# The first stages of an encoder layer: a buffer claimed at once, sums copied ahead of squares, first half blocks interleaved, late transposes on another engine

## The chip, the cores and the metric

The kernel runs on one core of one Trainium2 chip. The metric is device time in microseconds (us) of one execution. The core has TensorE (PE in the profile; its weight loads are PEld), VectorE (DVE), ScalarE (ACT), GpSimd (POOL) and SyncE (SP), each with its own instruction stream, and 16 DMA engines. SP's stream issues nearly all the loads and many stores; POOL's stream issues other stores and small memsets.

## The reference

One encoder layer over 1024 positions of width 2048, in float32, batch 1:

```python
mod = silu(c) @ w_ada + b_ada
shift, scale, gate = split(mod, 3)
h = rmsnorm(x, pre_g) * (1.0 + scale) + shift
q, k, v, gate_a, u, gate_p = split(h @ w_in)
y_a = windowed_gqa(q, k, v, rel_table, sink) * silu(gate_a)
y_p = multiscale_pool(u, w_pool_grp, pool_scale) * silu(gate_p)
g_a, g_p = split(sigmoid(h @ w_merge + b_merge), 2)
o = (g_a * (y_a @ w_br_attn) + g_p * (y_p @ w_br_pool)) @ w_out
return x + gate * rmsnorm(o, post_g)
```

Only the path to the first columns of `h @ w_in` matters here: the factors of rmsnorm (one per row of x), the scale and the shift (one per column of x), and the first block products.

## The kernel before

**Products.** A float32 operand is split in a high and a low part (`whi`, `wlo`; B11h, B11l and so on), and a product is hi by hi, lo by hi and hi by lo, three matmuls of 128x128 by 128x512. Most of the kernel computes blocks of 256 columns with seven products instead of eight (`strassen`, L212; its matmuls are at L237): the products X, V, Z and others are read from PSUM (the accumulators' memory) by ACT or DVE into sums of the same names.

**The ramp.** The first eight blocks of columns of `w_in` are computed from the first half of x's columns (k-tiles 0 to 3, two pairs j = 0 and 1) before the rest is ready. Blocks 0 to 3 are plain: each has four quarters "11", "21", "12" and "22" (first digit: half of the block's columns; second: half of the rows of x), and each quarter six matmuls per j (`plain_block`, L805, matmuls PB at L814). Their results are copied to `held` tiles (`hold`) or to `c` tiles (`put_by`, L825) and stored to `ramp_d` in DRAM, `held` by SP (`store_held`, L823), `c` by POOL. Blocks 4 to 7 go through `strassen` (`ramp_gen`).

**What comes ahead of the products.** x arrives as `xt` tiles by rows and is transposed on PE (`turn_part`, XT at L486); the transposes are taken from PSUM by `take_turned` (ACT at L494, or DVE). `raw_operands` makes the operands B11h and so on of transposed x with the column factors, in which the row factors and the shift are still missing. The column factors come from sums over `w_ada` on PE (`row_sums`, GEMV at L523; the loads `ada` at L546), whose result ACT copies to `acc` (L527); PE transposes `acc` (PM at L507), and DVE makes `modc`. `modulation` (GEMV at L583) does the same for later columns.

**Row factors.** `square_of` squares a part of x's rows and sums it into `ssq_x`, on ACT (L446) or DVE. `factors` makes `rstd` from the sums, DVE makes eight diagonal pieces `diag` of it, PE spreads them over partitions (RB at L474), and ACT copies the result to `rb` (L475). With `rb` DVE makes the shift-free sums (`sums_unshifted`, L688; `sums_over`), and `put_shifted` adds the shift: from there on the operands are those of h.

**What sets the order.** Instructions that pass through `keep` stand on their engine in the order of the program; a scheduler places the others between them. Tiles of a pool share buffers: the pool `xa` has five buffers of one tag, for which `rb`, four `held` tiles and later `ada` tiles ask. A buffer goes to a tile at its first writing in the scheduled order, not where the tile is named; a tile that gets a used buffer waits until the last use of the old tile is over. A memset of one element by POOL is the kernel's way of claiming a buffer early. In `run`, the steps of the list `at` are called at the given product of a strassen block; `side` steps (here `late_sums`) after products by their count.

The steps around `rb` in the main program, in their order: `factors()`, `put_by(2, "11")`, `low = [wide_weights(3, j) ...]`, `whole_block(2, "21")`, `put_by(2, "21")`, `whole_block(2, "12")`, `spread_factors(low)`, `put_by(2, "12")`, `scale_row` of 0 to 3, block 3 "11", `sums_unshifted()`, block 3 "21", the row sums of the shifts, `sums_over()`, block 2 "22", and then the column step `g[4]()` of the shifts with PM.

Of the kernel before, what the change touches and what calls it, by code (L numbers as in the profile page):

```python
# [15 lines left out]
AF = mybir.ActivationFunctionType  # L16
# [27 lines left out]
def encoder_layer(ctx: ExitStack, tc: tile.TileContext, x, c, table, w_ada, b_ada, pre_g,  # L44
# [409 lines left out]
    rb = xa.tile([P, 2, 512], F32, tag="xa", name="rb")  # L454
    held = {(i, nt): xa.tile([P, 2, 512], F32, tag="xa", name=uid("held")) for i in range(2) for nt in "12"}
# [7 lines left out]
    def spread_factors(then):  # L463
        diags = []
        for s in range(2):
            diags.append(ev.tile([P, 512], F32, tag="ev", name=uid("diag")))
            for m in range(4):
                keep(nc.vector.tensor_scalar(diags[s][:, m * P:(m + 1) * P], ident, rstd[:, 4 * s + m:4 * s + m + 1],
                                             None, op0=ALU.mult))
        for step in then:  # L470
            step()
# [321 lines left out]
    def wide_weights(i, j):  # L793
# [3 lines left out]
        keep(nc.scalar.activation(hi, src, AF.Copy))  # L797
# [7 lines left out]
    def plain_block(i, blk, j, tag=None):  # L805
# [4 lines left out]
        if j == 0:  # L810
            opened[i, blk] = bank(tag, "PB")
        for n in range(6):
            kh, w, m = ((0, whi, 0), (0, wlo, 0), (1, whi, 0), (1, wlo, 0), (0, whi, 1), (1, whi, 1))[n]
# [41 lines left out]
    def turn_next(tags):  # L855
        s, ks = rounds.popleft()
        turn_part(s, ks, tags)
        return [partial(take_turned, s, k, False) for k in ks]
# [11 lines left out]
    low00 = wide_weights(0, 0)  # L870
    g[4]()
    low00()
# [4 lines left out]
    plain_block(0, "11", 0, "sc")  # L877
    plain_block(0, "21", 0, "sc")
    turn_part(1, (0, 1), ("at", "at"))
    raw_operands(0, 1, True)  # L880
    for k in range(2):
        take_turned(1, k, k == 1)
    plain_block(0, "12", 0, "mm")
    plain_block(0, "22", 0, "mm")
# [6 lines left out]
    for si in range(8):  # L891
        square_of(si, 0, si % 2 == 1)
# [6 lines left out]
    raw_operands(1, 1)  # L899
    keep(nc.scalar.activation(ep.tile([P, 1], F32, name="root"), eps_t, AF.Sqrt))  # L900
# [37 lines left out]
    factors()  # L938
    put_by(2, "11")
# [4 lines left out]
    spread_factors(low)  # L944
# [37 lines left out]
    late_takes = [turn_next(("sc", "sc")), turn_next(("at", "at"))]  # L982
# [41 lines left out]
    for n, i in enumerate(range(AHEAD_PAIRS, RAMP)):  # L1024
        at = [(1, partial(second_raws, n - 2))] if n > 1 else []
        if n == 0:
            at.extend(((1, lambda: ramp_raws(7, (0, 1))), (2, partial(take_late, 0)), (3, fill_last),
                       (4, partial(take_late, 1))))
# [930 lines left out]
```

## Time and profile before

| what | value |
|---|---|
| median of 3 runs | 2104.43 us (2101.16 to 2106.51) |
| profiled execution | 2103.02 us, its span 2101.2 us |
| mean clock granted to TensorE | 0.997 |
| PE busy | 2074.6 us, 99% |
| DVE busy | 1557.0 us, 74% |
| ACT busy | 1112.0 us, 53% |
| POOL busy | 42.7 us, 2% |
| DMA | 227 GB/s mean over the span |

The span runs from the first to the last instruction that the profile shows. A row of an engine gives its start, its length, line, operation, output and inputs, their shape, and how often it stands in a row; the bracket at its end is the idle time ahead of it and what ended that. In the chain of waits each step is followed back to what released it. The clock is given as a share of full speed.

### The profile page before, as it was taken

The page shows a single profiled execution, that of the slowest core. Times are in us where ns is not written, and L with a number is a line of the kernel's source. Part 1 is how long each engine was busy: PE and PEld are TensorE (multiplying, and loading weights), DVE is VectorE, ACT ScalarE, POOL GpSimd, SP SyncE. Part 2 cuts the span into 40 slices and gives each one's busy share as a digit, 9 for nine tenths or more (in the row PEclk, how much of TensorE's full clock was granted, in tenths as well). Part 3 has the DMA queues.
Part 4 walks back from the last instruction along what each step waited for, and adds up shares of the span by engine and source line. Part 5 has one row for each costly group of instructions (what it writes and reads, how often), then busy time and mean ns, then how long its engine had stood idle before and what let it go on. Part 6 is the DMA issues. An engine that isn't in the chain of part 4 may idle for free.

```text
span 2101.2 us, 29057 instructions
## 1 busy us (share of the span) xinstructions
PE 2074.6 (99%) x9524; PEld 1704.4 (81%) x9524; DVE 1557.0 (74%) x2804; ACT 1112.0 (53%) x2122; POOL 42.7 (2%) x142
## 2 busy tenths in 40 slices
PE   8899999999999999999999999999999999999998
PEld 5578888788888888888888888888888888888886
DVE  5589777777456776777777678857857977889667
ACT  5574444444574634666665444333645645768654
POOL 1100000000000000000000000010000000000000
PEclk9999999999999999999999999999999999999999
DMA  9868787897575467654544577675755566786896
GB/s 350 308 220 291 261 256 227 282 297 252 170 249 187 151 226 265 223 173 157 187 165 154 165 232 233 213 241 173 251 159 172 171 199 200 231 302 206 295 337 244
DMA packets 303393, 476.62 MB, mean 227 GB/s; under 512 B 24322, under 2 KB 140650, under 8 KB 303240
## 3 DMA queue, kind: packets, MB, share of 16 engines
q1 hardware_dynamic: 297616, 459.89, 66.6%
q0 software_dynamic: 4560, 12.75, 1.6%
q10 hardware_dynamic: 1064, 2.11, 0.3%
q8 instruction: 75, 1.23, 0.3%
q14 instruction: 78, 0.64, 0.1%
HBM read 346.70 MB, written 130.05 MB: 227 GB/s over the span
## 4 chain that ended last, share of the span: by engine, by line
PE 93%; DMA 3%; DVE 2%; ACT 1%; issue 0%; POOL 0%; DVEq 0%; ACTq 0%; SPq 0%; POOLq 0%
PE Z L237 31%; PE X L237 20%; PE V L237 20%; PE Z L1666 2%; PE Z L1668 2%; PE Z L1667 2%; PE X L1666 1%; PE V L1666 1%; PE V L1668 1%; PE X L1668 1%; PE X L1667 1%; PE V L1667 1%; PE PT L1376 1%; PE PB L814 1%; PE PV L1387 0%; DMA xt<-in_x_dram 0%
## 5 line engine op out<-in xcount | busy, mean ns | idle before, releaser
L96 ACT ACTIVATE whi<-raw 128x512 fp32r<-128x512 f32 (+1 forms) x528 | 314.9, 601 | 490.7 <-PE Z L237 249.8
L97 DVE TENSOR_TENSOR wlo<-raw,whi 128x512 fp32r<-128x512 f32 (+1 forms) x528 | 340.2, 650 | 150.3 <-PE Z L237 109.6
L97 DVE TENSOR_TENSOR wlo<-wr,whi 128x512 fp32r<-128x512 f32 x224 | 150.9, 689 | 52.4 <-ACT whi L96 49.4
L96 ACT ACTIVATE whi<-wr 128x512 fp32r<-128x512 f32 x224 | 138.6, 629 | 86.4 <-DVE wlo L97 30.8
L103 DVE TENSOR_TENSOR raw<-raw,raw 128x512 f32<-128x512 f32 x76 | 52.5, 691 | 91.9 <-DMA raw<-in_w_merge_dram 60.2
L96 ACT ACTIVATE whi<-ws 128x512 fp32r<-128x512 f32 (+1 forms) x88 | 53.0, 603 | 74.0 <-PE X L237 60.0
L237 PE MATMUL V<-T4h,whi 128*128 128x512 f32 x328 | 89.4, 391 | 2.0 <-ACT whi L96 2.0
L237 PE MATMUL Z<-T1h,whi 128*128 128x512 f32 x328 | 90.3, 392 | 0.8 <-ACT u L251 0.8
L237 PE MATMUL Z<-B22h,whi 128*128 128x512 f32 x328 | 89.9, 392 | 0.0
L237 PE MATMUL X<-B21h,whi 128*128 128x512 f32 x328 | 89.6, 391 | 0.1
L237 PE MATMUL V<-T3h,whi 128*128 128x512 f32 x328 | 89.5, 391 | 0.2 <-ACT c L828 0.2
L237 PE MATMUL X<-B11h,whi 128*128 128x512 f32 x328 | 89.6, 391 | 0.0
L237 PE MATMUL Z<-T2h,whi 128*128 128x512 f32 x328 | 89.0, 390 | 0.4 <-ACT Z L293 0.3
L237 PE MATMUL X<-B11l,whi 128*128 128x512 f32 x328 | 89.1, 390 | 0.0
L237 PE MATMUL Z<-T2h,wlo 128*128 128x512 f32 x328 | 88.9, 390 | 0.2 <-DVE wlo L97 0.2
L237 PE MATMUL V<-T4h,wlo 128*128 128x512 f32 x328 | 89.0, 390 | 0.0
L237 PE MATMUL Z<-T1l,whi 128*128 128x512 f32 x328 | 89.0, 390 | 0.0
L237 PE MATMUL Z<-B22l,whi 128*128 128x512 f32 x328 | 88.9, 390 | 0.0
L237 PE MATMUL X<-B21l,whi 128*128 128x512 f32 x328 | 88.9, 390 | 0.0
L237 PE MATMUL V<-T3l,whi 128*128 128x512 f32 x328 | 88.9, 390 | 0.0
L237 PE MATMUL X<-B11h,wlo 128*128 128x512 f32 x328 | 88.8, 390 | 0.0
L237 PE MATMUL V<-T4l,whi 128*128 128x512 f32 x328 | 88.8, 390 | 0.0
(418 smaller groups left out, 4913.4 us busy)
## 6 DMA issues: line engine op xcount, KB each, us to landing
part<-part_d SPq DMA_DIRECT2D x136, 256.0 KB, 4.8
ada<-in_w_ada_dram SPq DMA_DIRECT2D x128, 256.0 KB, 5.1
raw<-in_w_merge_dram SPq DMA_DIRECT2D x64, 512.0 KB, 5.4
wr<-ws_dS SPq DMA_DIRECT2D x60, 512.0 KB, 5.2
raw<-in_w_in_dram SPq DMA_DIRECT2D x56, 512.0 KB, 4.3
wr<-in_w_out_dram SPq DMA_DIRECT2D x48, 512.0 KB, 5.1
proj_d<-part SPq DMA_DIRECT2D x68, 256.0 KB, 2.4
sw<-in_w_out_dram SPq DMA_DIRECT2D x64, 256.0 KB, 4.9
```

Source lines behind the costliest of these rows:

```text
L96: ins = (nc.scalar.activation(hi, src, AF.Copy), nc.vector.tensor_tensor(lo, src, f32(hi), ALU.subtract))
L97: nc.vector.tensor_tensor(lo, src, f32(hi), ALU.subtract))
L103: return (eng or nc.vector).tensor_tensor(o, a, b, ALU.add)
L237: nc.tensor.matmul(ps, w_[:, i], op[mov][j][m_], start=fresh and i == 0 and n == 0, stop=i == nj - 1 and n == 2, skip_group_check=True)
L814: keep(nc.tensor.matmul(opened[i, blk], w[:, kh, nt * P:(nt + 1) * P], mov[kh][m], start=j == n == 0, stop=j == 1 and n == 5, skip_group_c ...
L1376: nc.tensor.transpose(pt[:, i * P:(i + 1) * P], p[:, i * P:(i + 1) * P], ident)
L1666: nc.tensor.matmul(pb, hi, w[0], start=first, stop=False, skip_group_check=True)
L1667: nc.tensor.matmul(pb, lo, w[0], start=False, stop=False, skip_group_check=True)
L1668: nc.tensor.matmul(pb, hi, w[1], start=False, stop=last, skip_group_check=True)
```

## The change

A memset of one element by POOL claims `rb`'s buffer ahead of the four `held` tiles. The diagonals are made right behind `factors()`, half of them by ACT. The first `whi` is made by DVE. `plain_block` takes a list of its matmuls (`part`) and has another order of them; the first two pairs of quarters of block 0 are interleaved, with the third part of the first pair behind the transposes of the second half of the rows. Of the squares ahead of the second scale's sums, those of row tiles 2 to 7 move behind `raw_operands(1, ...)`. The late transposes are taken by DVE, and the steps `take_late` and `fill_last` of the ramp's first strassen block move from the products 2, 4 and 3 to 4, 5 and 6.

```diff
@@ -452,6 +452,7 @@
         square_of(si, 1, by_vector, xts[si, 2 + by_vector])
 
     rb = xa.tile([P, 2, 512], F32, tag="xa", name="rb")
+    nc.gpsimd.memset(rb[:, 0, 0:1], 0.0)
     held = {(i, nt): xa.tile([P, 2, 512], F32, tag="xa", name=uid("held")) for i in range(2) for nt in "12"}
 
     def factors():
@@ -460,15 +461,19 @@
         keep(nc.scalar.activation(t[:, 1], t[:, 0], AF.Sqrt, bias=eps_t, scale=1.0 / D))
         keep(nc.vector.reciprocal(rstd, t[:, 1]))
 
-    def spread_factors(then):
-        diags = []
+    diags = []
+
+    def factor_diagonals():
         for s in range(2):
             diags.append(ev.tile([P, 512], F32, tag="ev", name=uid("diag")))
             for m in range(4):
-                keep(nc.vector.tensor_scalar(diags[s][:, m * P:(m + 1) * P], ident, rstd[:, 4 * s + m:4 * s + m + 1],
-                                             None, op0=ALU.mult))
-        for step in then:
-            step()
+                at, factor = diags[s][:, m * P:(m + 1) * P], rstd[:, 4 * s + m:4 * s + m + 1]
+                if m % 2:
+                    keep(nc.scalar.activation(at, ident, AF.Copy, scale=factor))
+                else:
+                    keep(nc.vector.tensor_scalar(at, ident, factor, None, op0=ALU.mult))
+
+    def spread_factors():
         for s, tag in enumerate(SEEDED):
             ps = bank(tag, "RB")
             keep(nc.tensor.matmul(ps, ones, diags[s], start=True, stop=True))
@@ -790,11 +795,14 @@
 
     weights0 = {}
 
-    def wide_weights(i, j):
+    def wide_weights(i, j, by_vector=False):
         hi, lo = (wp.tile([P, 2, 256], F32R, tag=t, name=uid(t), bufs=4) for t in ("whi", "wlo"))
         src = wide[i // 2, j][:, :, i % 2 * 256:i % 2 * 256 + 256]
         weights0[i, j] = hi, lo
-        keep(nc.scalar.activation(hi, src, AF.Copy))
+        if by_vector:
+            keep(nc.vector.tensor_copy(hi, src))
+        else:
+            keep(nc.scalar.activation(hi, src, AF.Copy))
         return partial(low_weights, lo, src, hi)
 
     def low_weights(lo, src, hi):
@@ -802,15 +810,15 @@
 
     opened = {}
 
-    def plain_block(i, blk, j, tag=None):
+    def plain_block(i, blk, j, tag=None, part=range(6)):
 
         nt, s = int(blk[0]) - 1, int(blk[1]) - 1
         whi, wlo = weights0[i, j]
         mov = (op["B11"][j], op["B21"][j]) if s == 0 else (right[j], op["B22"][j])
-        if j == 0:
+        if tag:
             opened[i, blk] = bank(tag, "PB")
-        for n in range(6):
-            kh, w, m = ((0, whi, 0), (0, wlo, 0), (1, whi, 0), (1, wlo, 0), (0, whi, 1), (1, whi, 1))[n]
+        for n in part:
+            kh, w, m = ((0, whi, 0), (1, whi, 0), (0, wlo, 0), (1, wlo, 0), (0, whi, 1), (1, whi, 1))[n]
             keep(nc.tensor.matmul(opened[i, blk], w[:, kh, nt * P:(nt + 1) * P], mov[kh][m], start=j == n == 0,
                                   stop=j == 1 and n == 5, skip_group_check=True))
 
@@ -852,10 +860,10 @@
 
     rounds = deque((s, ks) for s in range(2) for ks in ((4, 5), (6, 7)))
 
-    def turn_next(tags):
+    def turn_next(tags, by_vector=False):
         s, ks = rounds.popleft()
         turn_part(s, ks, tags)
-        return [partial(take_turned, s, k, False) for k in ks]
+        return [partial(take_turned, s, k, by_vector) for k in ks]
 
     def whole_block(i, blk):
         plain_block(i, blk, 0, "sc" if blk[1] == "1" else "mm")
@@ -867,28 +875,35 @@
     g[2]()
     small_vectors()
     g[3]()
-    low00 = wide_weights(0, 0)
     g[4]()
-    low00()
+    wide_weights(0, 0, True)()
     turn_part(0, (0, 1), SEEDED)
     raw_operands(0, 0, True)
     for k in range(2):
         take_turned(0, k, k == 1)
-    plain_block(0, "11", 0, "sc")
-    plain_block(0, "21", 0, "sc")
+    PAIR = (("11", "sc"), ("21", "sc"))
+    for blk, tag in PAIR:
+        plain_block(0, blk, 0, tag, range(2))
+    for blk, _ in PAIR:
+        plain_block(0, blk, 0, None, range(2, 4))
     turn_part(1, (0, 1), ("at", "at"))
+    for blk, _ in PAIR:
+        plain_block(0, blk, 0, None, range(4, 6))
     raw_operands(0, 1, True)
     for k in range(2):
         take_turned(1, k, k == 1)
-    plain_block(0, "12", 0, "mm")
-    plain_block(0, "22", 0, "mm")
+    PAIR = (("12", "mm"), ("22", "mm"))
+    for blk, tag in PAIR:
+        plain_block(0, blk, 0, tag, range(2))
+    for blk, _ in PAIR:
+        plain_block(0, blk, 0, None, range(2, 6))
     turn_part(1, (2, 3), ("at", "at"))
     turn_part(0, (2, 3), SEEDED)
     for n in (1, 0):
         for k in (2, 3):
             take_turned(n, k, k == 3)
     wide_weights(1, 0)()
-    for si in range(8):
+    for si in range(2):
         square_of(si, 0, si % 2 == 1)
     g = row_sums(scz, scales[1], partial(scale_columns, 1), 2)
     for step in g[:4]:
@@ -897,6 +912,8 @@
     wide_weights(0, 1)()
     raw_operands(1, 0)
     raw_operands(1, 1)
+    for si in range(2, 8):
+        square_of(si, 0, si % 2 == 1)
     keep(nc.scalar.activation(ep.tile([P, 1], F32, name="root"), eps_t, AF.Sqrt))
     plain_block(1, "11", 0, SEEDED[0])
     plain_block(1, "21", 0, SEEDED[1])
@@ -936,12 +953,15 @@
     whole_block(2, "11")
     norm_row(7)
     factors()
+    factor_diagonals()
     put_by(2, "11")
     low = [wide_weights(3, j) for j in range(2)]
     whole_block(2, "21")
     put_by(2, "21")
     whole_block(2, "12")
-    spread_factors(low)
+    for step in low:
+        step()
+    spread_factors()
     put_by(2, "12")
     for si in range(4):
         scale_row(si)
@@ -979,7 +999,7 @@
     whole_block(3, "22")
     put_by(3, "22")
     first_given(2)
-    late_takes = [turn_next(("sc", "sc")), turn_next(("at", "at"))]
+    late_takes = [turn_next((tag, tag), True) for tag in ("sc", "at")]
     put_shifted("B21", lambda j: block_of(j, 1, 0), shift(1))
     early.close()
 
@@ -1024,8 +1044,8 @@
     for n, i in enumerate(range(AHEAD_PAIRS, RAMP)):
         at = [(1, partial(second_raws, n - 2))] if n > 1 else []
         if n == 0:
-            at.extend(((1, lambda: ramp_raws(7, (0, 1))), (2, partial(take_late, 0)), (3, fill_last),
-                       (4, partial(take_late, 1))))
+            at.extend(((1, lambda: ramp_raws(7, (0, 1))), (4, partial(take_late, 0)), (5, partial(take_late, 1)),
+                       (6, fill_last)))
         if i == RAMP - 1:
             at.append((4, partial(get_parts, SECOND[0], ev)))
         run(ramp_gen((0, 1), i, None, False, given=() if n else given), side, range(7), at)
```

All lines behind L452 move: the squares stay at L446, and with the change the copies to `rb` stand at L480 (before L475), the diagonals on ACT at L472, transposes at L491 (L486), takes at L499 (L494), the sums at L528 (L523), `acc` at L532 (L527), `whi` of the ramp at L805 (L797), `put_by`'s copies at L836 (L828).

ACT's order around the second scale, before: takes of the transposes (xT), the weights of block 1, four squares, and then `acc`.

```order
L494 ACTIVATE xT_196<-XT_474 128x512 [waits PE_49]
L494 ACTIVATE xT_194<-XT_484 128x512 [waits PE_49]
L797 ACTIVATE whi_498<-wide_171 128x512 [waits DMAHW6_49]
L446 ACTIVATE xt_163,ssq_x<-xt_163 128x512 [waits DMAHW2_49,DMAHW1_49]
L446 ACTIVATE xt_167,ssq_x<-xt_167 128x512 [waits DMAHW4_49,DMAHW3_49]
L446 ACTIVATE xt_173,ssq_x<-xt_173 128x512
L446 ACTIVATE xt_177,ssq_x<-xt_177 128x512 [waits DMAHW0_49]
L527 ACTIVATE acc_527<-GEMV_510 128x256 [waits PE_49]
L797 ACTIVATE whi_536<-wide_248 128x512 [waits DMAHW7_49]
```

And with the change, from the same take on (the raw operands B11h to B22h are those of j = 1):

```order
L499 ACTIVATE xT_197<-XT_475 128x512 [waits PE_49]
L499 ACTIVATE xT_195<-XT_485 128x512 [waits PE_49]
L805 ACTIVATE whi_499<-wide_172 128x512 [waits DMAHW6_49]
L446 ACTIVATE xt_164,ssq_x<-xt_164 128x512 [waits DMAHW2_49,DMAHW1_49]
L532 ACTIVATE acc_522<-GEMV_505 128x256 [waits PE_49]
L805 ACTIVATE whi_531<-wide_249 128x512 [waits DMAHW7_49]
L684 ACTIVATE B11h_217<-xT_195,modc 128x512 [waits DVE_49,Activation_49,Pool_49]
L684 ACTIVATE B21h_221<-xT_0_199,modc 128x512 [waits DVE_49,Pool_49]
L684 ACTIVATE B12h_229<-xT_197,modc 128x512 [waits Pool_49]
L684 ACTIVATE B22h_225<-xT_1_200,modc 128x512
L446 ACTIVATE xt_168,ssq_x<-xt_168 128x512 [waits DMAHW4_49,DMAHW3_49]
```

Three of the four squares have moved behind `acc` and the four raw operands.

ACT's order around `rb`, before. A bracket names the semaphores on which an instruction waits; DMAHW5 is a count of transfers.

```order
L460 ACTIVATE rms<-rms,eps_t 128x8 [waits DVE_49]
L828 ACTIVATE c_760<-PB_740 128x512 [waits PE_49]
L797 ACTIVATE whi_763<-wide_274 128x512
L797 ACTIVATE whi_766<-wide_276 128x512
L828 ACTIVATE c_782<-PB_769 128x512 [waits PE_49]
L475 ACTIVATE rb<-RB_810 128x512 [waits DMAHW5_49,PE_49,Activation_49]
L475 ACTIVATE rb<-RB_813 128x512 [waits PE_49]
L828 ACTIVATE c_816<-PB_785 128x512
L478 ACTIVATE xt_254<-xt_254,rstd 128x512 [waits DMAHW2_49,DVE_49]
```

The same place with the change:

```order
L461 ACTIVATE rms<-rms,eps_t 128x8 [waits DVE_49]
L472 ACTIVATE diag_761<-ident,rstd 128x128 [waits DVE_49]
L472 ACTIVATE diag_761<-ident,rstd 128x128
L472 ACTIVATE diag_766<-ident,rstd 128x128 x2
L836 ACTIVATE c_771<-PB_741 128x512 [waits PE_49]
L805 ACTIVATE whi_774<-wide_275 128x512
L805 ACTIVATE whi_777<-wide_277 128x512
L836 ACTIVATE c_793<-PB_780 128x512 [waits PE_49]
L480 ACTIVATE rb<-RB_811 128x512 [waits PE_49]
L480 ACTIVATE rb<-RB_814 128x512 [waits PE_49]
L836 ACTIVATE c_817<-PB_796 128x512
```

Four pieces of the diagonals have come to ACT, and the first copy to `rb` waits for PE alone.

ACT's order in the ramp's first strassen block, before (`p`, `u` and `c` are results of the block's products, xT are the late transposes taken from PSUM, `raw` the weights from DRAM):

```order
L293 ACTIVATE Z_1041<-X_1040 128x512 [waits PE_49,Activation_49]
L251 ACTIVATE p_234_1056<-V_1042 128x512 [waits DMASW7_49,PE_49]
L494 ACTIVATE xT_352<-XT_1015 128x512
L494 ACTIVATE xT_356<-XT_1016 128x512 [waits DMAHW3_49]
L96 ACTIVATE whi_1075<-raw_668 128x256 [waits DMAHW7_49]
L251 ACTIVATE u_236_1069<-Z_1041 128x512 [waits PE_49]
L725 ACTIVATE B22h_208<-xT_192,modc 128x512
L725 ACTIVATE B22h_224<-xT_1_199,modc 128x512
L332 ACTIVATE c_1085<-X_1040 128x512 [waits PE_49]
L494 ACTIVATE xT_360<-XT_1025 128x512
L494 ACTIVATE xT_1_363<-XT_1026 128x512
L96 ACTIVATE whi_1091<-raw_668 128x256 [waits Activation_49]
```

And with the change:

```order
L293 ACTIVATE Z_1042<-X_1041 128x512 [waits PE_49,Activation_49]
L251 ACTIVATE p_234_1057<-V_1043 128x512 [waits DMASW6_49,PE_49]
L96 ACTIVATE whi_1070<-raw_669 128x256 [waits DMAHW7_49]
L96 ACTIVATE whi_1086<-raw_669 128x256 [waits Activation_49]
L96 ACTIVATE whi_1105<-raw_669 128x256 [waits Activation_49]
L96 ACTIVATE whi_1126<-raw_672 128x256 [waits DMAHW0_49,DVE_49,PE_49]
L251 ACTIVATE u_236_1068<-Z_1042 128x512 [waits PE_49]
L96 ACTIVATE whi_1132<-ws_1130 128x256 [waits DVE_49,PE_49]
L332 ACTIVATE c_1080<-X_1041 128x512 [waits DMASW7_49,PE_49]
L96 ACTIVATE whi_1174<-raw_669 128x256 [waits DVE_49,PE_49,Activation_49]
L96 ACTIVATE whi_1189<-raw_672 128x256 [waits DVE_49,PE_49,Activation_49]
```

The four takes and two B22h have gone from between the weights `whi`, which follow each other.

## The prediction

> **What bounds the kernel now.** I read the head of the page first, then the table of stages, then the list of what TensorE (PE) waited for, and last the rows of PE, ScalarE (ACT), VectorE (DVE) and SyncE's queue (SPq) in the stages where PE is not full.
>
> ```profile
> span 2101.2 us, 29057 instructions
> PE 2074.6 (99%) x9524; PEld 1704.4 (81%) x9524; DVE 1557.0 (74%) x2804; ACT 1112.0 (53%) x2122; POOL 42.7 (2%) x142
> ```
>
> PE is idle for 26.6 us of 2101.2, so a change of order can win only there, or where PE is busy but slow. The stages (length, then the busy time of PE, PEld, DVE, ACT and POOL, the clock granted to PE, DMA's share, GB/s):
>
> ```profile
> 60.00:70.00 10.00, 6.14 (x44) 2.95 (x36) 7.06 (x12) 7.69 (x14) 2.70 (x15) 1.00 1.08 369
> 70.00:80.00 10.00, 8.69 (x37) 7.60 (x38) 9.26 (x21) 5.91 (x12) 0.54 (x1) 0.66 0.50 175
> 90.00:100.00 10.00, 8.04 (x31) 4.25 (x31) 6.18 (x14) 5.50 (x13) 1.11 (x2) 0.83 1.08 357
> 300.00:2101.00 1801.00, 1791.05 (x8191) 1487.49 (x8189) 1337.44 (x2361) 952.52 (x1802) 29.52 (x69) 1.00 0.66 218
> ```
>
> After 300 us PE lacks 10 us of 1801, and the change touches nothing there. The rest is nearly all in the first 100 us, where two stages also have a lower clock (0.66 and 0.83). The list of waits puts two of the places behind ACT (us in total, times, longest):
>
> ```profile
> PE PM L507 <- ACT acc L527: 7.6, 3, 5.2
> PE PB L814 <- ACT B12h L679: 0.7, 1, 0.7
> ```
>
> PE's own rows give their times, with the idle time before a row in brackets:
>
> ```profile
> 13.51 0.50 PE L814 MATMUL PB<-B11h,whi 128*128 128x512 f32 x1 [1.00 <-ACT B11h L679]
> 21.77 1.91 PE L486 MATMUL XT<-ident,xt 128*128 128x128 f32 x16
> 23.61 1.93 PE L523 MATMUL GEMV<-ada,scz 128*32 128x256 f32 x32
> 27.48 0.44 PE L507 MATMUL PM<-ident,acc 128*128 128x128 f32 x2 [1.94 <-ACT acc L527]
> 52.27 1.88 PE L474 MATMUL RB<-diag,ones 128*128 128x512 f32 x4
> 65.76 0.39 PE L814 MATMUL PB<-B22l,whi 128*128 128x512 f32 x1
> 92.89 0.73 PE L237 MATMUL V<-T4h,whi 128*128 128x512 f32 x2 [1.96 <-ACT whi L96]
> ```
>
> And why ACT was late in the big one:
>
> ```profile
> 24.62 0.62 ACT L446 ACTIVATE xt<-xt 128x512 f32<-128x512 f32 x1
> 62.31 1.08 ACT L475 ACTIVATE rb<-RB 128x512 f32<-128x512 f32 x2 [11.97 <-DMA ramp_d<-held]
> 62.94 2.74 DVE L688 SCALAR_TENSOR_TENSOR xT<-xT,modc,rb 128x512 f32<-128x512 f32 x4 [12.02 <-ACT rb L475]
> 70.66 0.60 ACT L527 ACTIVATE acc<-GEMV 128x512 f32<-128x512 f32 x1
> 74.28 0.41 ACT L96 ACTIVATE whi<-raw 128x256 fp32r<-128x256 f32 x1
> 86.82 0.60 ACT L293 ACTIVATE Z<-X 128x512 f32<-128x512 f32 x1
> ```
>
> The row factors (RB) were on PE at 52.27, but ACT could not copy them to `rb` until a store of a `held` tile had landed: `rb` had been given that tile's buffer. ACT stood for 11.97 us, and DVE behind it for 12.02. From there both work through one chain, from `rb` at 62.31 to the copy Z at 86.82: 24.5 us in which each waits only for the other. PE ran out of prepared work at 65.99 (the row at 65.76 and 0.23, the step from one product to the next), and paid 5.2 us.
>
> Then the chain that ended last, where it follows PE (start, us, what). It tells busy time at half speed from the same work at full speed:
>
> ```profile
> 71.31 1.12 PE PM L507 x4
> 72.42 1.71 PE XT L486 x8
> 74.13 4.23 PE PB L814 x12
> 78.36 0.87 PE XT L486 x8
> 79.23 2.76 PE PB L814 x12
> 94.69 1.86 PE GEMV L583 x8
> 96.55 2.12 PE Z L237 x6
> 98.68 1.39 PE X L237 x6
> 100.06 2.71 PE GEMV L583 x24
> 104.36 0.44 PE PM L507 x4
> ```
>
> **The change part by part.** The sum counts how much earlier PE comes to the block product X at 98.68; behind it the engines' order is soon the old one.
>
> *First half blocks and the second scale.* The first `whi` goes to DVE (a CAST of 128x512, of which there is no row; between 0 and the 0.62 of ACT's square I take 0.62, the nearest in size). ACT then starts B11h as soon as the transposes end, and I take 0.24 of the 1.00 as won: PE starts at 13.27. It may wait 0.3 and 0.2 for the second moving half of each pair, and four products now stand behind the transposes and cover the 0.7 for B12h. 24 products at 0.23 are 5.5, eight transposes 0.9, fills 0.2: this part ends at 20.4, 1.4 before 21.77. Then 1.84 of transposes (23.61 - 21.77) and 1.93 of sums bring PE to 24.2, if the transfers are there:
>
> ```profile
> 13.56 4.29 SPq L546 DMA_DIRECT2D ada<-in_w_ada_dram  x8
> DMA to landing us min/median/max: 3.0/5.0/5.7
> ```
>
> The last of eight is issued near 17.4 and lands by 23.1: barely in time. ACT has one square ahead of `acc` instead of four and is free when PE ends, so PM starts at 24.6 instead of 27.48: **2.9 us**. The three squares moved on each of ACT and DVE (1.9 us) lie beside some 20 us of products whose operands are prepared before them. What they could delay is the factors:
>
> ```profile
> 47.27 0.19 DVE L459 TENSOR_REDUCE rms<-ssq_x 128x8 f32<-128x32 f32 x1
> 49.63 1.29 DVE L106 TENSOR_TENSOR wlo<-wide,whi 128x512 fp32r<-128x512 f32 x2
> ```
>
> DVE was through with the diagonals at 49.63. Four of the eight are on ACT now, which by half of DVE's time for them (0.8) makes it 48.8. PE comes to RB at 52.27 - 2.9 = 49.4, so the 2.9 passes with half a microsecond to spare. Its ends are 0 (the factors, which wait for x to land, hold RB at 52.27) and 3.4.
>
> *The buffer.* ACT's copy to `rb` now has only PE to wait for. The first bank is done 0.7 after RB starts, so `rb` starts at 50.1 instead of 62.31. `acc` is 8.35 later (70.66 - 62.31), or behind PE's sums of the shifts; these end one block of twelve products (2.8) ahead of 65.99 - 2.9 = 63.1. Either way `acc` is there first, and the **5.2 us** go. The memset is one small instruction of POOL at the start, where nothing waits for it. Four `ada` tiles, where three did, wait for stores of `held` in SP's queue:
>
> ```profile
> 51.47 3.13 SPq L823 DMA_DIRECT2D ramp_d<-held  x4
> 54.69 3.93 SPq L187 DMA_DIRECT2D raw<-in_w_in_dram  x4
> 58.67 1.64 SPq L500 DMA_DIRECT2D ada<-in_w_ada_dram  x2
> DMA to landing us min/median/max: 7.0/7.8/8.4
> ```
>
> The first store lands between 58.5 and 59.9, where the first load is due at 58.67: up to 1.2 us on SP, on loads that PE wants 30 us later. Three stores `ramp_d<-c` (256 KB each) come to stand before 60 instead of after 64, while DMA is full (1.08 at 369 GB/s): 0.7 us each, at most 2.1 for the weights `raw` of the ramp.
>
> *The clock.* Behind the 5.2 us gap PM, eight transposes and twelve products took 1.12 + 1.71 + 4.23 = 7.06; the same work takes 0.44 + 0.87 + 2.76 = 4.07 at full speed. Of these 3.0 us I take **2.9**. Behind the gap of 1.96 eight sums and six products took 3.98, against 0.90 (a third of 2.71) and 1.39: **1.6 us** of 1.7. Both go with their gaps.
>
> [...]
>
> *The ramp's first block.* The gap of 1.96 came from ACT, which had four takes of transposes and two B22h ahead of the weights of the fourth product (some 0.6 each as the copies above). They now stand behind those weights, or on DVE, busy for 6.2 of 10 us there. Smaller waits of this block (for `V`, `Z` and the third weights) are some 0.9 in all, by my estimate from the idle time of the stages (1.96 in the last one, 0.65 in the one before). New times: `rb` at 50.1 and the chain of 24.5 put the copy Z at 74.6, up to 76.7 with the 2.1 above; PE, which was at its product 0.6 after that copy, comes at 86.82 + 0.6 - 11.6 = 75.8 (2.9, 5.2, 2.9 and the wait of about 0.6 there). So PE waits between 0 and 0.9; I take 0.4, and of 2.9 there remain **2.5 us**.
>
> Sum: 2.9 + 5.2 + 2.9 + 1.6 + 2.5 = 15.1 us. The profiled execution took 2103.0 (its span and 1.8 around it), the median of the runs 2104.4, 1.4 more; the shift holds for both. **2104.4 - 15.1 = 2089.3**. Less than 0.3% (6.3 us) a measurement of this kernel cannot well tell from no change.
>
> **The rivals.**
> (1) *The factors hold RB.* DVE and ACT have the 1.9 us of squares late, and RB goes at 49.63 + 1.9 instead of 49.4: 2.1 of the early 2.9 are lost, 2091.4. For it: x is still landing and DMA is full; against it: the row at 47.27 shows the end of a queue that DVE worked off, not when x landed, and half the diagonals are gone from it.
> (2) *Late weights.* The chain asks for the first `raw` 12 us behind `rb` (74.28 - 62.31), at 62.1. It is issued at 54.69 and lands by 63.1 at 8.4, or 65.2 with POOL's stores ahead of it. If the following ones are 3 us late and PE waits, a gap of that size brings half the clock back (1.6): 15.1 - 4.6, 2093.9.
> (3) *Another wait in place of the old one.* The chain starts early but meets something as late, such as the memsets of T1 on POOL, which now stand behind two more stores. Then only the early 2.9 is won: 2101.5. Against it: the last of these stores waits for a block that ACT copies directly ahead of T1, so T1 is late by one issue.
> (4) *Slower, by SP's queue.* The last two `ada` loads now stand ahead of the weights of the ramp's fourth block, and wait for PE's 24 sums, which ended at 102.8 and now end at 87.7. The weights are issued by 89 and land 3.0 to 8.4 later, by 97.4. DVE wants them at 112.19 - 15.1 = 97.1:
>
> ```profile
> 112.19 0.42 DVE L106 TENSOR_TENSOR ws<-raw 128x256 f32<-128x256 f32 x1
> ```
>
> Each microsecond past that is DVE's, and soon PE's. It decides only from 15 us on: for 2111 they would have to land near 118, 29 us after the issue. Nothing in the rows takes a third of that.
>
> **How the numbers follow.** The forecast has 0.62; its own range is 2085.5 to 2092.5 (the ends of the early part, 0 to 0.9 of wait at Z, and 2 between runs). Rival 1 has 0.12, rival 2 0.14, rival 3 0.08, rival 4 0.04. Faster by over 0.3% (below 2098.1) are the forecast and rivals 1 and 2: 0.88. The same: 0.08. Slower: 0.04. From 2085 to 2097 lie nearly all of the first three.
>
> **What would show it.** Right: ACT does not wait for `ramp_d<-held`, and copies `rb` near 50; PM of the second scale near 24.6; PM of the shifts with no idle time ahead of it; a clock of 1.00 from 60 to 100 us; the X of 98.68 near 83.6. Wrong: a gap of PE over 1 us between 45 and 90 us, behind `diag` (rival 1), `raw` (2) or POOL (3), or between 95 and 115 us behind `raw` (4); and a half clock without a gap would say that the two are not tied as I have it.

## The result, and the profile after

The changed kernel took 2088.48 us (median of six runs, 2086.43 to 2090.74) beside 2103.01 for the kernel before in the same six rounds: a ratio of 0.9926, 95% interval 0.9911 to 0.9941, 14.5 us. Forecast were 2089.3 and 15.1. The profiled execution took 2088.67 with a span of 2086.9, 14.3 less than before. The sum of the terms holds; two of the terms mean something other than I took them to mean, which only the experiments show.

The head of the page, and the same stages of the table by time as in the prediction (length; busy time of PE, PEld, DVE, ACT, POOL; clock; DMA share; GB/s):

```profile
span 2086.9 us, 29056 instructions
PE 2070.1 (99%) x9524; PEld 1702.2 (82%) x9524; DVE 1556.7 (75%) x2805; ACT 1111.0 (53%) x2121; POOL 42.6 (2%) x143
...
60.00:70.00 10.00, 10.00 (x61) 7.77 (x54) 8.91 (x21) 6.49 (x13) 1.03 (x9) 1.00 1.07 379
70.00:80.00 10.00, 9.81 (x51) 7.94 (x50) 7.36 (x14) 9.65 (x20) 1.59 (x3) 1.00 1.09 369
90.00:100.00 10.00, 10.00 (x46) 8.25 (x45) 9.34 (x22) 8.55 (x18) 0.00 (x0) 1.00 1.03 354
```

PE is idle for 16.8 us instead of 26.6, and busy for 4.5 less with the same 9524 matmuls. That is about the 3.0 and 1.7 of the half clock in the prediction's rows; the clock is now 1.00 in all three stages.

PE's rows after. The steps to compare are the four PM (the first scale's, the second's, the shifts', and that of the later columns, group 2), RB, and the first block product X:

```profile
11.71 0.44 PE L512 MATMUL PM<-ident,acc 128*128 128x128 f32 x2 [0.48 <-ACT acc L532]
13.74 0.50 PE L822 MATMUL PB<-B11h,whi 128*128 128x512 f32 x1 [0.72 <-ACT B11h L684]
21.05 1.91 PE L491 MATMUL XT<-ident,xt 128*128 128x128 f32 x16
25.35 0.44 PE L512 MATMUL PM<-ident,acc 128*128 128x128 f32 x2 [0.53 <-ACT acc L532]
50.17 1.88 PE L479 MATMUL RB<-diag,ones 128*128 128x512 f32 x4
63.90 0.60 PE L512 MATMUL PM<-ident,acc 128*128 128x128 f32 x4
72.42 0.71 PE L237 MATMUL X<-B11h,whi 128*128 128x512 f32 x2
76.50 0.73 PE L237 MATMUL Z<-T2h,whi 128*128 128x512 f32 x2 [0.19 <-ACT Z L293]
88.95 0.60 PE L512 MATMUL PM<-ident,acc 128*128 128x128 f32 x4
```

The rows of before at the same steps, as far as the prediction did not show them:

```profile
11.19 0.44 PE L507 MATMUL PM<-ident,acc 128*128 128x128 f32 x2 [0.48 <-ACT acc L527]
71.31 1.12 PE L507 MATMUL PM<-ident,acc 128*128 128x128 f32 x4 [5.16 <-ACT acc L527]
82.78 0.74 PE L237 MATMUL X<-B11h,whi 128*128 128x512 f32 x2
104.20 0.60 PE L507 MATMUL PM<-ident,acc 128*128 128x128 f32 x4
```

The last of these PM comes 15.25 us earlier (104.20 - 88.95). The largest wait of PE between RB and it is now 0.19. ACT has `rb` at once, and `acc` stands finished (61.26 and 0.60) well before PE asks for it at 63.90:

```profile
51.23 0.60 ACT L480 ACTIVATE rb<-RB 128x512 f32<-128x512 f32 x1 [0.18 <-PE RB L479]
61.26 0.60 ACT L532 ACTIVATE acc<-GEMV 128x512 f32<-128x512 f32 x1
```

### The profile page after: what moved, and what is told of

Read it like the earlier page. It is cut to its first block, busy times and chain, and to the rows that moved or that the text cites. A ratio compares the mean times of both kernels' runs of the same rounds, so it can differ in the third digit from the quotient of the medians.

```text
span 2086.9 us, 29056 instructions
## 1 busy us (share of the span) xinstructions
PE 2070.1 (99%) x9524; PEld 1702.2 (82%) x9524; DVE 1556.7 (75%) x2805; ACT 1111.0 (53%) x2121; POOL 42.6 (2%) x143
## 4 chain that ended last, share of the span: by engine, by line
PE 91%; DMA 4%; DVE 3%; ACT 1%; issue 1%; SPq 0%; DVEq 0%; ACTq 0%; POOL 0%; POOLq 0%
PE Z L237 30%; PE V L237 20%; PE X L237 20%; PE Z L1686 2%; PE Z L1688 2%; PE Z L1687 2%; PE PB L822 1%; PE X L1686 1%; PE X L1687 1%; PE X L1688 1%; PE V L1687 1%; PE V L1686 1%; PE V L1688 1%; DMA raw<-in_w_in_dram 1%; PE PT L1396 1%
```

## How the runs are compared

The first 12 us differ also between kernels whose code is the same up to there: the first PM came between 11.01 and 12.54 us in the 14 profiles, at 11.19 in before and at 12.45 in filled_gaps, with waits of up to 1.8 us for the loads of `ada` ahead of it. The rest of the program, from the fourth PM to the end of the span, took 1997.0 us before, 1997.95 after, and 1996.5 to 2001.9 in the others. So I compare stages, each a difference of two starts of PE's rows: from the first to the second PM, from RB to the third PM, and from the third to the fourth. From the second PM to RB it is 24.7 to 24.8 us everywhere but in two runs, told below.

| kernel | median us | ratio to before, interval | PM 1 to 2 | RB to PM 3 | PM 3 to 4 |
|---|---|---|---|---|---|
| before | 2103.0 to 2105.0 | 1 | 16.29 | 19.04 | 32.89 |
| the change | 2088.48 | 0.9926, 0.9911 to 0.9941 | 13.64 | 13.73 | 25.05 |
| buffer_alone | 2092.15 | 0.9942, 0.9930 to 0.9954 | 16.30 | 13.73 | 25.56 |
| all_but_buffer | 2100.92 | 0.9987, 0.9978 to 0.9996 | 13.65 | 21.52 | 28.60 |
| all_but_takes | 2095.41 | 0.9957, 0.9945 to 0.9970 | 13.65 | 13.72 | 29.31 |
| all_but_early | 2092.76 | 0.9947, 0.9935 to 0.9959 | 16.00 | 13.72 | 25.06 |
| takes_act_late | 2090.42 | 0.9927, 0.9912 to 0.9942 | 13.65 | 13.73 | 25.08 |
| takes_dve_soon | 2088.91 | 0.9920, 0.9907 to 0.9933 | 15.01 | 13.72 | 25.56 |
| squares_ahead | 2092.16 | 0.9933, 0.9920 to 0.9947 | 17.57 | 13.73 | 25.07 |
| filled_gaps | 2103.94 | 0.9994, 0.9984 to 1.0005 | 15.99 | 18.18 | 31.29 |
| three_gaps | 2103.14 | 1.0000, 0.9992 to 1.0009 | 16.29 | 19.84 | 32.37 |
| sums_covered | 2087.92 | 0.9931, 0.9918 to 0.9945 | 13.90 | 13.73 | 25.53 |
| halves_apart | 2091.32 | 0.9943, 0.9930 to 0.9955 | 17.04 | 13.73 | 25.07 |
| diag_one | 2091.03 | 0.9940, 0.9927 to 0.9952 | 16.41 | 13.73 | 25.06 |

By stages the change won 2.65 + 5.31 + 7.84 = 15.80; the late first PM (11.71 against 11.19) took 0.52 of it.

## The experiments

**buffer_alone**: the kernel before with one line.

```diff
     rb = xa.tile([P, 2, 512], F32, tag="xa", name="rb")
+    nc.gpsimd.memset(rb[:, 0, 0:1], 0.0)
```

> The kernel before, with the memset that claims the buffer of rb and nothing else of the change. Theory (the buffer carries most of it by itself): ACT copies rb near 53.3 us, PE finds acc ready, so the gap of 5.16 ahead of PM and the half clock behind it go: the block product X that stood at 82.78 starts near 74.5, 8.3 earlier. The chain from rb is 9.0 earlier, so the gap of 1.96 ahead of V shrinks by 0.7 to about 1.3; if that is too short to lower the clock, 1.6 more are won: 10.6 us faster than before in all, 9.0 if the clock still halves. Rival (the parts need each other): with the second scale's sums and the squares as they were, the factors or another store hold rb; PM keeps a gap of 2 us or more, and less than 6 us are won.

PE's and ACT's rows:

```profile
52.49 1.88 PE L475 MATMUL RB<-diag,ones 128*128 128x512 f32 x4
66.22 0.60 PE L508 MATMUL PM<-ident,acc 128*128 128x128 f32 x4
75.83 0.71 PE L237 MATMUL X<-B11h,whi 128*128 128x512 f32 x2
81.71 0.61 PE L237 MATMUL V<-T4h,whi 128*128 128x512 f32 x2
91.78 0.60 PE L508 MATMUL PM<-ident,acc 128*128 128x128 f32 x4
...
53.55 0.60 ACT L476 ACTIVATE rb<-RB 128x512 f32<-128x512 f32 x1 [2.98 <-PE RB L475]
```

The gap ahead of PM and the half clock are gone (the clock is 1.00 from 66 to 98 us), as the theory has it. (X is at 75.83 and not at 74.5 because all 16 last transposes stand ahead of it here; before, eight of them stood among its products.) But the gap ahead of V is gone too, which I had put at 1.3: the last PM is 12.4 earlier than before (104.20 - 91.78), most of the change by one memset; the medians give 12.0, more than the 10.6 that I had at best. Nothing in the edit touches the late takes; the scheduler has placed ACT's work anew. ACT's order there in this kernel:

```
L293 ACTIVATE Z_1042<-X_1041 128x512
L96 ACTIVATE whi_1076<-raw_669 128x256
L96 ACTIVATE whi_1092<-raw_669 128x256
L251 ACTIVATE p_234_1057<-V_1043 128x512
L495 ACTIVATE xT_353<-XT_1016 128x512
L495 ACTIVATE xT_357<-XT_1017 128x512
```

Two weights of the next products now stand ahead of the takes, which are where they were in the code.

**all_but_buffer**: the change without that memset.

```diff
-    nc.gpsimd.memset(rb[:, 0, 0:1], 0.0)
```

> The changed kernel without the memset; all else of the change stays. Theory (the wait for the store swallows what is won ahead of it): RB is on PE near 50.2 as with the change, but ACT copies rb near 62.3, when the store of held lands, and PM stands at 71.3 as before: the gap ahead of it is 7.3 instead of 5.16, the clock halves behind it, and the 2.1 us of the first stages are lost again. The late takes still win the 1.96 gap, small waits and the second half clock, about 4 us: 4 us faster than before, 10.3 slower than the change. Rival (the parts add up): PM at 69.2, 8.2 slower than the change, 6.1 faster than before.

```profile
49.86 1.88 PE L478 MATMUL RB<-diag,ones 128*128 128x512 f32 x4
71.38 1.12 PE L511 MATMUL PM<-ident,acc 128*128 128x128 f32 x4 [7.64 <-ACT acc L531]
82.84 0.72 PE L237 MATMUL X<-B11h,whi 128*128 128x512 f32 x2 [0.87 <-ACT c L835]
...
62.38 1.09 ACT L479 ACTIVATE rb<-RB 128x512 f32<-128x512 f32 x2 [11.65 <-DMA ramp_d<-held]
```

The theory: RB is 2.4 earlier than before, PM is not (71.38 against 71.31), and the gap has grown to 7.64. Early work without the buffer is worth nothing: the store's landing sets `rb`. What is left, 3.2 us by the medians, comes behind the third PM (28.60 against 32.89). (The profiled execution itself, 2103.81 us, was no faster than before: far behind the ramp it lost more than it had won, as told below.)

**all_but_takes**: the change with the late takes as before.

```diff
-    late_takes = [turn_next((tag, tag), True) for tag in ("sc", "at")]
+    late_takes = [turn_next((tag, tag)) for tag in ("sc", "at")]
...
-(4, partial(take_late, 0)), (5, partial(take_late, 1)), (6, fill_last)
+(2, partial(take_late, 0)), (3, fill_last), (4, partial(take_late, 1))
```

> The changed kernel with the late transposes taken by ACT at the products 2 and 4, and fill_last at 3, as before. Theory: the chain behind rb is 11.1 earlier than before and PE 10.4, so the gap ahead of V comes back, but smaller than 1.96: about 1.3, with 0.3 of small waits; 1.6 us slower than the change, and the clock stays at 1.00 behind so short a gap. Rival (any gap there halves the clock): 3.3 us slower than the change, with a clock under 0.9 between 82 and 90 us. Third way (the rest of the change had already taken the gap): no gap, no difference.

```profile
82.37 0.73 PE L237 MATMUL V<-T4h,whi 128*128 128x512 f32 x2 [1.97 <-ACT whi L96]
84.45 1.93 PE L588 MATMUL GEMV<-ada,scz 128*32 128x512 f32 x8
```

The rival: the gap is back in full (1.97, as before with 1.96), and the eight sums behind it take 1.93 instead of 1.06, with a mean clock of 0.67 from 82 to 86 us. The stage behind the third PM is 4.26 longer. ACT's order shows why the same takes at the same places cost nothing in buffer_alone:

```
L293 ACTIVATE Z_1042<-X_1041 128x512
L251 ACTIVATE p_234_1057<-V_1043 128x512
L499 ACTIVATE xT_353<-XT_1016 128x512
L499 ACTIVATE xT_357<-XT_1017 128x512
L96 ACTIVATE whi_1076<-raw_669 128x256
L251 ACTIVATE u_236_1070<-Z_1042 128x512
```

Here the takes are ahead of the weights again. So what PE waits for is set by where the scheduler puts a few copies that no one has pinned. Why it puts them ahead here and behind in buffer_alone, no run shows.

**takes_act_late** undoes the engine alone (the first `-`/`+` pair of the diff above), **takes_dve_soon** the place alone (the second pair).

> The changed kernel with the late transposes taken by ACT, but at the changed places (products 4 and 5, fill_last at 6): the engine alone is undone. Theory (place in the order decides: weights of the next products ahead of the takes): the four weights whi come behind the first two at ACT's rows 93 to 99 with two takes and two copies among them, so the third is some 2 us later than with the change; PE waits 0 to 1 us for it, the clock stays full: 0 to 1 us slower than the change. Rival (ACT is simply overfull there, DVE must take them): the gap of 2 us ahead of V comes back with its half clock, 3.6 us slower.

> The changed kernel with the late transposes taken by DVE, but at the places of before (products 2 and 4, fill_last at 3): the place alone is undone. ACT still makes the four weights in a row ahead of B22h. Theory: no gap ahead of V, PE as with the change within 0.3 us: no difference in time. Rival (DVE's own chain is late by four takes, 2.7 us, so the low parts wlo come late): a gap of 1 us or more ahead of the products X, V or Z between 77 and 84 us, caused by DVE.

V in takes_act_late, V in takes_dve_soon, and ACT in takes_dve_soon:

```profile
79.03 0.61 PE L237 MATMUL V<-T4h,whi 128*128 128x512 f32 x2
```

```profile
80.50 0.62 PE L237 MATMUL V<-T4h,whi 128*128 128x512 f32 x2
...
66.00 0.42 ACT L96 ACTIVATE whi<-raw 128x256 fp32r<-128x256 f32 x1 [0.66 <-DMA raw<-in_w_in_dram]
```

On the gap both theories hold: there is none ahead of V in either. The stages are 25.08 and 25.56 against 25.05. The second is 0.51 longer, more than the 0.3 that I allowed it, but not by the takes: ACT waited 0.66 for the load of the ramp's first weights `raw`, ahead of the late takes, and PE's V and Z came later by it. (In sums_covered, told below, ACT waited 0.68 there, and the stage is 25.53.) Either half of this edit is enough, since with either the weights stand ahead of the takes. In takes_dve_soon the first stage was 1.4 longer: the sums, which started 0.6 earlier than in the change, took 3.25 instead of 1.93, by my estimate for their loads: SP issued these from 14.67 on instead of 14.09.

```profile
22.29 3.25 PE L528 MATMUL GEMV<-ada,scz 128*32 128x256 f32 x32
```

**all_but_early**: first half blocks, first `whi` and squares as before.

```diff
-    wide_weights(0, 0, True)()
+    low00 = wide_weights(0, 0)   # ahead of g[4](), low00() behind it
...
-    (the two interleaved PAIRs)
+    plain_block(0, "11", 0, "sc")   # and "21", "12", "22", in the old order of matmuls
...
-    for si in range(2):
+    for si in range(8):
...
-    for si in range(2, 8):
-        square_of(si, 0, si % 2 == 1)
```

> The changed kernel with the first half blocks, the first whi and the squares as before. Theory: PM of the second scale at 27.5 instead of 25.35, RB at 52.3 instead of 50.17, and everything behind it 2.1 us later up to the end: 2.1 us slower than the change. Rival (something behind RB has slack): the loads and the chain from rb leave PE waiting anyway by 0.5 us or more with the early RB, and less than 1.5 us of the 2.1 reach the ramp's first block product.

```profile
22.83 1.91 PE L491 MATMUL XT<-ident,xt 128*128 128x128 f32 x16
28.54 0.44 PE L512 MATMUL PM<-ident,acc 128*128 128x128 f32 x2 [1.95 <-ACT acc L532]
```

The 16 transposes start 10.29 us behind the first PM (22.83 - 12.54) instead of 9.34, and PM 5.71 behind these instead of 4.30: 0.95 for the half blocks, 1.41 for the squares, 2.36 together where I expected 2.1. RB was another 1.56 later, which I had not foreseen: behind the gap of 1.95 ahead of PM the clock was 0.50 from 29.10 to 32.51, and behind a gap of 1.94 in before it stayed at 1.00. Nothing behind RB had slack to give back (13.72 and 25.06, as with the change), so the rival is out.

**squares_ahead**, **halves_apart**, **diag_one** each undo one piece: the last two parts of the diff above (the squares), its first two parts (the half blocks with the first `whi`), and of the diagonals

```diff
-                if m % 2:
-                    keep(nc.scalar.activation(at, ident, AF.Copy, scale=factor))
-                else:
-                    keep(nc.vector.tensor_scalar(at, ident, factor, None, op0=ALU.mult))
+                keep(nc.vector.tensor_scalar(at, ident, factor, None, op0=ALU.mult))
```

> The changed kernel with all eight squares ahead of the second scale's sums, as before; the half blocks stay interleaved. [...] Rival (the loads of the sums or the factors hold the place anyway): RB at most 0.5 us later than with the change.

> The changed kernel with the first half blocks and the first whi as before; the squares stay behind. Theory: the waits for B11h (0.72 or 1.0), the second moving half and B12h (0.7) come back: the 16 transposes start 10.3 to 10.6 us behind the first PM instead of 9.34, and all behind is 0.95 to 1.25 us later. Rival (the sums then wait less for their loads): half of it or less reaches RB.

> The changed kernel with all eight pieces of the diagonals on DVE, at the changed place. Theory: DVE makes them from 47.8 to 49.5, PE comes to RB at 50.2: no wait, RB 38.5 us behind the first PM as with the change, no difference. Rival (the split over two engines carries the early RB): PE waits 0.3 us or more ahead of RB.

In these three profiles the first eight transposes were slow, as here in diag_one:

```profile
12.64 1.92 PE L488 MATMUL XT<-ident,xt 128*128 128x128 f32 x8
```

1.92 instead of 1.04: PE came to full rate only near 18 to 19 us (a product PB took 0.63 in them at 18.1 to 18.5, and 0.39 or 0.40 at 19.3 to 20.4), so the first stage (16.41 to 17.57) says nothing on an edit worth 1 us. What can be read is what follows: from the 16 transposes to PM it took 5.72 in squares_ahead (23.59 to 29.31) and 4.30 in halves_apart, so the squares are worth 1.42, where the rival had RB 0.5 later at most. halves_apart alone settles nothing on the half blocks. In diag_one PE did not wait for RB and came to it 24.82 behind PM, as with the change (24.82): splitting the diagonals over two engines was worth nothing here. Their new place in the program was not undone by itself; in before, too, DVE made them directly behind `rstd` (at 48.06, `rstd` being at 47.82).

**filled_gaps** and **three_gaps**: the kernel before with matmuls of no use where PE is idle, to hold up the clock and nothing else.

```diff
     put_by(2, "22")
+    warm(20)
     g[4]()
...
-                       (4, partial(take_late, 1))))
+                       (4, partial(take_late, 1)), (4, partial(warm, 8))))
```

In three_gaps another `warm(8)` stands ahead of the second scale's PM, and the matmuls write to banks "at" and "sc". In filled_gaps they write to a bank in which the ramp's sums get their starting values, and change that part of the computation; only its times are used.

> The kernel before with matmuls of no use put into its two gaps: 20 of 128x128 ahead of PM of the shifts, 8 ahead of the V that follows the late takes; what the products wait for is as late as before. Theory (the half clock comes from PE's idle time): both waits stay, PM at 71.3, but the clock is 1.00 from 60 to 100 us; of the 5.2 and 2.0 nothing is won, of the slow work behind them 2.9 and 1.7: 4.6 us faster than before. Rival (the clock falls for another cause, such as the burst of DMA or of ACT and DVE at that time): the clock still shows 0.66 and 0.83 in the stages 70 to 80 and 90 to 100, and the time is that of before within 1 us.

> The kernel before with matmuls of no use in three gaps: 8 of 128x128 ahead of PM of the second scale, 20 ahead of PM of the shifts, 8 ahead of the V behind the late takes; they write to banks of which nothing is read. What the products wait for is as late as before. Theory, from the run with two gaps filled, where X came 20.47 us behind the copy rb, to the hundredth as in the kernel before: the chain behind rb, not PE's clock, sets X. So the first half clock's 2.9 come back as a wait of about 2 us ahead of X, X stands at 82.8 as before (rb near 62.3), and only the second half clock is won: PM of group 2 at 102.6 instead of 104.2, 1.6 us faster than before. Rival (the two terms of my sum hold each by itself): X at 79.9, 4.6 us faster than before.

PE and ACT in filled_gaps, then in three_gaps:

```profile
68.56 4.62 PE L835 MATMUL WARM<-ident 128*128 128x128 f32 x40
84.45 0.73 PE L237 MATMUL X<-B11h,whi 128*128 128x512 f32 x2 [2.04 <-ACT c L828]
...
63.98 1.09 ACT L475 ACTIVATE rb<-RB 128x512 f32<-128x512 f32 x2 [11.07 <-DMA ramp_d<-held]
```

```profile
83.74 0.73 PE L237 MATMUL X<-B11h,whi 128*128 128x512 f32 x2 [2.05 <-ACT c L828]
...
63.27 1.09 ACT L475 ACTIVATE rb<-RB 128x512 f32<-128x512 f32 x2 [12.77 <-DMA ramp_d<-held]
```

With the gap ahead of PM filled, the clock behind it is 1.00 from 70 to 78 us in both, where it was 0.54 and 0.60 in before (70 to 74, 74 to 78): that half clock did come with PE's idle time. But this gains nothing there, and of the 4.6 us that I expected of filled_gaps none shows in its times. X starts 20.47 behind `rb` in both (84.45 - 63.98, 83.74 - 63.27), as in before (82.78 - 62.31) and, to 0.01, in all_but_buffer. PE at full clock only arrives 2.0 earlier and waits. In three_gaps the clock is 0.50 in its turn behind this new wait, from 85.1 to 88.5 us, which eats most of what the filler had won of the second half clock; filled_gaps had a clock of 1.00 there, and won 1.6 behind the third PM (31.29 against 32.89). Neither kernel is faster than before by its times.

**sums_covered**: an attempt to better the change.

```diff
-        plain_block(0, blk, 0, None, range(2, 6))
+        plain_block(0, blk, 0, None, range(2, 4))
...
     for step in g[:4]:
         step()
+    for blk, _ in PAIR:
+        plain_block(0, blk, 0, None, range(4, 6))
     g[4]()
```

> The changed kernel with one more step: the last four products of block 0's second pair of quarters move from ahead of the transposes to behind the second scale's sums, so that PE works while ACT copies acc. Theory: the wait of 0.53 ahead of PM goes; the sums start 0.9 earlier and may wait for their loads instead, but the four products then stand behind that wait as well: PM of the second scale 13.1 us behind the first PM instead of 13.64, all else as with the change, 0.5 us faster, which the times cannot tell and the trace can. Rival (the loads hold the sums as long as they did, and the four products come on top): PM 13.6 to 14.5 behind the first, no gain or up to 0.9 slower.

The rival: 13.90 from the first PM to the second (11.29 to 25.19) against 13.64. The wait for `acc` is gone, and the sums start 10.23 behind the first PM (21.52) instead of 11.17, but they take 2.71 (to 24.23) instead of 1.93. By my estimate these 0.8 are a wait for their loads, though no row shows that wait by itself; the times of this kernel and the change cannot be told apart.

## Why the prediction was right

The time was right to 0.8 us, and the stages to 0.8 each; what a part does was in two places wrong. That the total came so near is in part luck: by the stages the change won 15.8, and 0.52 of the late first PM and 0.95 behind the fourth, which are in no term of the sum, took it down to 14.3.

*First half blocks and second scale, 2.9.* Measured 2.65 between the first two PM (16.29 to 13.64), and 2.13 by the times themselves (27.48 to 25.35), since the first PM was late by 0.52. The part up to the 16 transposes won 1.24 (21.77 - 11.19 = 10.58 to 21.05 - 11.71 = 9.34) where I had 1.4, and the rest up to PM 1.41, the squares, where I had 1.5. In the 1.24 are 0.95 for the half blocks (by all_but_early) and 0.28 for "0.24 of the 1.00 as won". But the 0.28 is not shown to be the work of the first `whi` on DVE: all_but_early and filled_gaps, which make it on ACT, wait 0.72 for B11h too. Their first PM is later, and so ACT waits 0.54 and 0.75 for `wide` there instead of 1.11. The first `whi` as CAST took 0.43, within my 0 to 0.62:

```profile
12.80 0.43 DVE L803 CAST whi<-wide 128x512 fp32r<-128x512 f32 x1
```

That the 2.9 would pass RB "with half a microsecond to spare" was right, with more to spare: DVE ended its four diagonals at 47.77 + 0.88 = 48.65, ACT the other four at 49.05, PE came at 50.17. Rival 1 did not occur.

```profile
47.77 0.88 DVE L474 TENSOR_SCALAR diag<-ident,rstd 128x128 f32<-128x128 f32 x4
```

*The buffer, 5.2.* Right: RB to PM became 5.31 shorter, in every kernel that has the memset and in none without. `rb` was 1.1 later than I had it (51.23 against 50.1), of which 0.8 is RB's own start and 0.3 that the copy comes 1.06 behind that start, not 0.7; nothing hung on it.

*The clock, 2.9.* The size held: from PM to X it took 11.47 before (82.78 - 71.31) and 8.52 after (72.42 - 63.90), 2.95 less. What I had wrong is that this is a price by itself, beside the 5.2. The filled runs show that in before the chain from `rb` to X, 20.47, was the bound whatever PE's clock; at full clock PE waited 2.0 instead. The 2.9 could be won only because `rb`, and the chain with it, came 11.1 earlier: X now stands 21.19 behind `rb` (72.42 - 51.23), 0.7 more than the chain needs, so here PE is the later of the two and its own terms count. The two terms have one cause, the early `rb`.

*The second half clock, 1.6, and the ramp's first block, 2.5.* The size held to 0.8: behind the third PM the change won 7.84, against 2.9 + 1.6 + 2.5 = 7.0 in my sum. Without the 2.95 up to X that leaves 4.89 against 4.1. The cause was half wrong. I put these on the late takes; buffer_alone has 7.33 of them with the takes untouched, and all_but_takes shows that without that edit 4.26 are lost again. What they share is whether the weights `whi` come ahead of the takes in ACT's order, which the edit assures and which buffer_alone had by the scheduler's choice. So this part is an insurance, not a gain that adds to the other.

*The rest.* Rival 2: PE did not wait for `raw` in the change, but it was near, as ACT's 0.66 and 0.68 in takes_dve_soon and sums_covered show: in these, which have the same loads there, 0.5 us was lost. Rival 3: POOL's memsets did make ACT wait for T4h, but only 0.97 us (ACT's T1h at 57.08), ahead of work that was early. Rival 4: the weights were issued at 90.28, 1.3 later than I had them, and DVE used them at 96.94 with no idle time ahead.

```profile
57.08 1.15 ACT L708 ACTIVATE T1h<-xT 128x512 fp32r<-128x512 f32 x2 [0.97 <-POOL T4h L657]
```

```profile
90.28 1.11 SPq L187 DMA_DIRECT2D raw<-in_w_in_dram  x2
...
96.94 0.42 DVE L106 TENSOR_TENSOR ws<-raw 128x256 f32<-128x256 f32 x1
```

By the fourth PM the change was 15.25 ahead, at the end 14.3. The 0.95 between lies in a stretch of 1997 us that none of the edits is meant to touch. The list of PE's waits has 1.5 us there in before and 2.5 after; the largest new ones are 0.8 for a `wlo` of DVE and 0.7 for the copy `k` of ACT ahead of the first scores of the attention. That wait is longer in other profiles, and longest in all_but_buffer (2001.9 from the fourth PM to the end), where it is 2.71 and the clock behind it 0.50:

```profile
859.95 0.38 PE L1372 MATMUL SCORE<-k,qhi 128*128 128x256 f32 x1 [2.71 <-ACT k L96]
...
856.81:860.22 3.41, 0.70 (x3) 0.19 (x2) 0.99 (x2) 1.84 (x4) 0.00 (x0) 1.00 0.89 302
860.22:863.63 3.41, 3.07 (x9) 2.48 (x9) 2.60 (x6) 3.07 (x6) 0.00 (x0) 0.50 0.83 262
```

Whether the edits have a part in these waits, one profile of each kernel does not show.

## What to carry to other kernels

When one copy stands for 12 us on a store's landing, look first at which buffer it was given: a tile that takes its buffer early costs one memset, and here gave 12 of 14.5 us. (By an estimate from the 4.26 us lost in all_but_takes, about 4 of the 12 came with the place that the scheduler chose for the weights.) A slow clock behind a gap, or a wait further on, is not a second gain until a run shows that nothing else bounds the same stretch; add up chains, not symptoms. Where a scheduler places unpinned work, an edit far away can move it, so compare the order of both kernels at the place that waits before crediting an edit there.

## What the runs showed of the hardware

In the first 110 us of these profiles five gaps of PE of about 2 us had a half clock (0.50) behind them, and four of the same length had a clock of 1.00. Where the half clock starts, and how long it lasts, is worked out from the mean clock of half microseconds (us; the row is the one behind the gap):

| kernel | row | gap | half clock from | length |
|---|---|---|---|---|
| before | V at 92.89 | 1.96 | 94.24 | 3.42 |
| all_but_takes | V at 82.37 | 1.97 | 83.32 | 3.42 |
| all_but_early | PM at 28.54 | 1.95 | 29.10 | 3.41 |
| filled_gaps | PM at 28.44 | 1.95 | 28.69 | 3.41 |
| three_gaps | X at 83.74 | 2.05 | 85.10 | 3.42 |
| before | PM at 27.48 | 1.94 | none | |
| buffer_alone | PM at 27.72 | 1.95 | none | |
| squares_ahead | PM at 29.31 | 1.95 | none | |
| filled_gaps | X at 84.45 | 2.04 | none | |

Of the longer gaps, the 5.16 ahead of PM in before (71.31) had a half clock from 70.35 on, while PE still waited, for 6.83; the 7.64 ahead of PM in all_but_buffer (71.38) had one from 68.33 on, also for 6.83. So the length of a gap alone does not tell whether the clock falls behind it: in before 1.94 did not and 1.96 did, in filled_gaps 1.95 did and 2.04 did not. What decides it, these runs do not show. In before the half clock behind the 1.96 made eight sums and six products take 3.98 instead of 0.90 + 1.39 = 2.29, 1.7 more. A gap of 2 us thus cost up to 1.7 us more here, or nothing, and an edit that removes such a gap removes that risk with it.

At the start of every run PE is slow too, though the clock column reads 1.00 there. In before, 16 sums of 128x256 took 3.25 at 6.11 us, where 32 took 1.93 at 23.61. The first eight transposes took 1.04 in eleven of the 14 profiles (starts from 11.28 to 12.82), as eight did later (1.04 at 16.76 in before), but 1.91 or 1.92 in squares_ahead, halves_apart and diag_one (starts from 12.23 to 12.64). In these three, products PB still took 0.63 at 18.06, 18.20 and 18.48, and 0.39 or 0.40 at 19.71, 19.31 and 20.42. One profile each cannot say whether their edits have a part in it.
